# Moving preparations of the gated-linear-attention stage behind the norm's column sums in a two-layer trunk

## The chip, the cores and the metric

The kernel runs on one core of a Trainium2 chip. The metric is the device time of one execution in microseconds (us); lower is better. Engines are named as in the profile: PE is TensorE, PEld its weight load, DVE is VectorE, ACT is ScalarE, POOL is GpSimd, SP is SyncE, which issues nearly all DMAs (SPq is its queue).

## The reference

Two layers on a sequence of 1024 positions and a width of 1024, all float32. Layer 0 mixes tokens by forgetting attention, layer 1 by gated linear attention (GLA); each mixer is followed by a SwiGLU channel mixer (hidden width 2816). Every part has an RMS norm in front, modulated by a conditioning vector. The part that matters here is the seam between layer 0's channel mixer and layer 1's GLA:

```
x = x + g2 * swiglu(h, ffn_w_in[0], ffn_w_out[0])           # end of layer 0
h = modulate(rms_norm(x, norm1_g[1]), sh1, sc1)             # the norm in front of GLA
proj = h @ w_in
q, k, v, r, a_lr = split(proj, ...)                          # widths 512, 512, 1024, 1024, 16
log_alpha = log_sigmoid(a_lr @ w_a2 + b_a) / 16              # the low-rank gate
b = cumsum(log_alpha over a chunk of 64)
A = tril((q * exp(b)) @ (k * exp(-b)).T)                     # per chunk and head
o = A @ v + (q * exp(b)) @ state                             # and the recurrence of the state
o = rms_norm_per_head(o) * g_o * silu(r)
```

## The kernel before

The activations lie transposed: eight tiles of 128 features by 1024 positions, worked on in two halves of 512 positions. Every product of two float32 matrices is made of three matmuls (`mm3`, lines 241 to 243) on a high part (`hi`, a rounded copy that ScalarE casts) and a low part (`lo`, the rest, a subtraction on VectorE or GpSimd). So each weight that is loaded is also split: `load_w` (line 194) issues one DMA into a raw buffer, two casts on ScalarE (line 206) and four subtractions of a quarter each (line 209), of which the first `lo_p` (3 unless said otherwise) run on GpSimd and the rest on VectorE. `load_w16` (line 212) does the same for 16 columns, after a memset of its tile on GpSimd (line 217).

Weights are taken from one long list, `loads`. `feed.next()` (line 234) first starts loads until `depth` (here 3) are in hand and then gives the oldest. Raw buffers come from a ring of three, `wr`; split weights from a ring of eight slots, `ws`. A buffer is used again when its last reader is done.

The seam runs like this. `last_chunk` multiplies the last four hidden tiles (products named `f0e...`) in two halves; after each of eight features VectorE adds the product to x (line 1062), ScalarE squares it (line 577), and additions gather the squares (line 584). `rms_cols` then sums the columns on TensorE with one-column matmuls (`sp`, line 529, remembered in `sp_ins`), takes the root on GpSimd (line 533), and `rms_rows` spreads it over partitions (`rb`, line 541, remembered in `rb_ins`). `norm_half` makes h1 for that half: a product on VectorE (te, lines 554 and 559), casts on ScalarE (lines 555, 560, 561) and the low part, on VectorE for even features (line 556) and on GpSimd for odd ones (line 562). While the second half waits for its sums, GLA's value product of the first positions can already run on the first half of h1: `gv_body` (line 1599) makes one value tile of two blocks of 128 positions and splits it out of PSUM (tile `gvt`).

GLA's set-up stands between: memsets of a mask pair (`atz`), of the gate weight tile `w2t` and of the low-rank activation tile `aT`, the load and split of the low-rank weight `gla_w_a2` (raw tile `w2raw`), and the loads of the first value weights (`wv`), the low-rank input columns (`aw`, by `load_w16`), the first gate weight (dv 0 of head 0) and the first key weight. `a_body` and `gate_z` (lines 1588 and 1611) use them; `r_proj` makes the gate products `gr`, `head_front` the key and query products `gk` and `gqp`.

The program is traced in the order of the text. A planner then sets the order of instructions on each engine by simulating it: an instruction whose inputs and buffers are ready may go ahead of earlier ones that aren't, and where several are ready the one traced first goes. `with tc.issue_after(ins)` adds an edge that keeps those instructions of its block that run on the engine of `ins` behind `ins` in that engine's order. `sp_ins[-1]` and `rb_ins[-1]` are TensorE instructions.

In between, `ada1(t)` advances the modulation of the second layer (`ada_pair`, line 350) by a given amount: loads on SyncE (line 361), a product on ScalarE (lines 375 and 377) that is kept behind the ScalarE instruction traced `ADA_LAG` (6) before the last one, and an add on GpSimd (line 379). `gv_body` calls it once for each value tile.

Of the kernel before, what the change touches and what calls it, by code (L numbers as in the profile page):

```python
# [9 lines left out]
F32 = mybir.dt.float32  # L10
# [43 lines left out]
def trunk(ctx, tc, x, c, ada_w, ada_b, norm1_g, norm2_g, ffn_w_in, ffn_w_out,  # L54
          fox_w_in, fox_b_f, fox_w_out, gla_w_in, gla_w_a2, gla_b_a, gla_g_o,
          gla_w_out, final_g, out, dbg=None, stop=None):
    nc = tc.nc
# [9 lines left out]
    def ps_rings(*counts):  # L67
        r, i = [], 0
        for n in counts:
            r.append(Ring(psp, [f"b{j}" for j in range(i, i + n)]))  # L70
            i += n
        assert i <= 8
        return r
# [35 lines left out]
    def psl(t, n=1):  # L109
        return slice(t * P, (t + n) * P)  # L110

    def run(g):
        for _ in g:
            pass
# [4 lines left out]
    def weave(a, ta, b, tb, lags=None):  # L119


        ca = cb = 0.0
        a_on = b_on = True
        bb = nc.cur_bb.bb.instructions
        hist = {e: [] for e in lags or ()}
        while a_on or b_on:
            n = len(bb)
            if a_on and (not b_on or ca * tb <= cb * ta):
                r = next(a, None)
                a_on = r is not None  # L130
                ca += r or 0.0
                for e, h in hist.items():
                    new = [i for i in bb[n:] if i.engine == ENG[e]]
                    h.append(new[-1] if new else h[-1] if h else None)
            else:
                r = next(b, None)
                b_on = r is not None
                cb += r or 0.0
                for e, h in hist.items():
                    if len(h) > lags[e] and h[-1 - lags[e]] is not None:  # L140
                        for i in bb[n:]:
                            if i.engine == ENG[e]:
                                tc.add_manual_dep(i, h[-1 - lags[e]].name, mybir.DependencyInfo(
                                    mybir.DependencyClass.NoSync, mybir.DependencyReason.DATA), reason="order")
# [17 lines left out]
    def split(hi, lo, src):  # L162
        nc.scalar.copy(hi, src)  # L163
        nc.vector.tensor_sub(lo, src, hi.bitcast(F32))  # L164

    wr = Ring(big, names[0:3])
    ws = Ring(big, names[3:9])
# [58 lines left out]
    class Weights:  # L226
# [4 lines left out]
            self.got = deque()  # L231
            self.depth = 3

        def next(self):
            while self.loads and len(self.got) < self.depth:
                f, *a = self.loads.popleft()
                self.got.append(f(*a))
            return self.got.popleft()

    def mm3(ps, ah, al, bh, bl, start, stop):  # L240
# [11 lines left out]
    def proj_tok(ps, w2, hs, t):  # L252

        ts_ = psl(t)
        for k in range(8):
            w = w2[k // 4]
            mm3(ps, hs[k].hi[:, ts_], hs[k].lo[:, ts_], w.hi[:, k % 4, :], w.lo[:, k % 4, :], k == 0, k == 7)
            yield 0.33
# [145 lines left out]
    class Pace:  # L404
# [6 lines left out]
        def __call__(self, t):  # L411
            self.at += t
            while self.q and self.at >= 0:
                w = next(self.q[0], None)
                if w is None:
                    self.q.popleft()
                else:
                    self.at -= w
            if not self.q:
                self.at = 0.0  # L420
# [7 lines left out]
    def ada1_queue(js, acc, raws_):  # L428
        r = Cycle(raws_)
        for j in js:  # L430
# [6 lines left out]
                            fill=1e30, base=0, channel_multiplier=1)  # L437
# [5 lines left out]
                            fill=0.0, base=0, channel_multiplier=-1)  # L443
# [201 lines left out]
    def v_loads(wmat, lo):  # L645
        return [(load_w, wmat[psl(k0, 4), lo:lo + 256], f"wv{lo}_{k0}") for k0 in (0, 4)]
# [97 lines left out]
    def ffn_loads(l):  # L744

        blk = lambda gr, ab, *after: (op_block, l, gr, ab, *after)
        sums = lambda gr, *after: (op_sums, l, gr, *after)
        outs = lambda k0, kc, n: [(op_out, l, k0, kc, m0, i) for i in range(n) for m0 in range(0, D, 512 // kc)]
        g, u = GROUPS[:2]
        four = (A11, A21, A22, A12)  # L750
        r = [(op_first, l, g, A11, (g, four), (u, (A11, A12))), blk(g, A12), blk(g, A21), blk(g, A22, (u, (A21, A22)))]
        gs = GROUPS[1:] + OGROUPS
        for a, n in zip(gs, gs[1:] + [None]):
            first, then = ((n, four[:2]),), ((n, four[2:]),)
            if n is None:
                first = then = ()
            if a == u:
                r += [blk(a, A11), blk(a, A12, *first), blk(a, A21), blk(a, A22, *then)]
                continue
            r += [blk(a, A11), sums(a, *first)]  # L760
            if a[0] < 2:
                r += [blk(a, A11), (op_a12, l, a), blk(a, A21, *then), blk(a, A22), blk(a, A12)]
            else:
                r += [(op_s2, l, a), blk(a, A21, *then), blk(a, A12), blk(a, A22), blk(a, "s")]
        return r + outs(NFH - 4, 4, 2 + l)

    Wg = gla_w_in[0]
    loads = v_loads(W, 2 * D)
# [5 lines left out]
        loads += [a + (ws, 4) for a in fox]  # L774
    loads += out_loads(fox_w_out[0], 0, 4) + 2 * out_loads(fox_w_out[0], 4, 4)
    loads += ffn_loads(0)
    loads += v_loads(Wg, 1024) + [(load_w16, Wg[:, 3072:3088], "aw")]
    for h in range(4):
        if h:
            loads += v_loads(Wg, 1024 + h * 256)  # L780
# [5 lines left out]
    feed = Weights(loads)  # L786
# [774 lines left out]
    atz = Views(take(1), 2, [4, P], "atz")  # L1561
# [7 lines left out]
    nc.vector.memset(rm.rearrange("p (n c) -> p n c", c=P)[:, :, 0:1], 0.0)  # L1569
    og_d = tc.dram_tile([8, P, S], F32, name="og_d")  # L1570
    pj, atr, kvr, opr, trr = ps_rings(3, 1, 1, 2, 1)
    for v_ in atz.v:
        nc.gpsimd.memset(v_, 0.0)
    S_t = big.tile([P, 2, 2, 256], FR, tag=s_slot, name="S_t")
    on_t = big.tile([P, 2, 2, 256], F32, tag=on_slot, name="on_t")
    QS = 128 ** -0.5

    w2raw = wr([64, 512], F32, "w2raw")
    nc.sync.dma_start(w2raw[0:16, :], gla_w_a2[0])
    nc.sync.dma_start(w2raw[32:48, :], gla_w_a2[0])  # L1580
    w2t = big.tile([P, 2, 512], FR, tag=wslot, name="w2t")
    nc.vector.memset(w2t.bitcast(F32), 0.0)
    for r0 in (0, 32):
        split(w2t[r0:r0 + 16, 0, :], w2t[r0:r0 + 16, 1, :], w2raw[r0:r0 + 16, :])
    aT = big.tile([P, S], FR, tag=aslot, name="aT")
    nc.vector.memset(aT.bitcast(F32), 0.0)

    def a_body(aw, hf, bt):
        ps = pj([P, HALF], F32, f"aps{hf}")
# [9 lines left out]
    def gv_body(h, wv, tp):  # L1599
        ps = pj([P, 2, 256], F32, f"gv{h}{tp}")  # L1600
        for i in range(2):
            run(proj_tok(ps[:, i, :], wv, h1, 2 * tp + i))
        ada1(5.1)
        v = vr([P, 2, 2, 256], FR, f"gvt{h}{tp}")
        split(v[:, 0], v[:, 1], ps)
        return v
# [201 lines left out]
    def r_proj(h, gs, done):  # L1808
        wr_ = [None, None]
        for hf, dv in ((0, 0), (0, 1), (1, 0), (1, 1)) if h else ((0, 0), (1, 0), (0, 1), (1, 1)):  # L1810
# [6 lines left out]
            done.add((dv, hf))  # L1817
            yield 0.01

    wv = [feed.next(), feed.next()]  # L1820
    aw = feed.next()
    vt = [gv_body(0, wv, 0)]
    with tc.issue_after(sp_ins[-1]):
        vt.append(gv_body(0, wv, 1))
    with tc.issue_after(rb_ins[-1]):
        bt = gate_tiles(0)
# [123 lines left out]
```

## Time and profile before

| | |
|---|---|
| median of 3 runs | 2423.62 us (2423.13 to 2425.41) |
| profiled execution, its own time | 2419.46 us |
| span of the profiled execution | 2417.7 us |
| granted TensorE clock, mean | 0.995 |
| PE busy | 2369.4 us (98%) |
| DVE busy | 1680.8 us (70%) |
| ACT busy | 1194.4 us (49%) |
| POOL busy | 1181.0 us (49%) |

The times in a profile's rows count from the start of the span. A row of a timeline has the start, the duration, the engine, the line of the kernel, the operation, and output and inputs by the program's names; idle time in front of it and what ended it stand in brackets. A row of a table by stages has the stage, its length, the busy time of PE, PEld, DVE, ACT and POOL with their numbers of instructions, the granted TensorE clock, the share of the DMA engines and GB/s.

### The profile page before, as it was taken

The numbers are of one execution on the slowest core, as the hardware profiler recorded it, in microseconds if no ns is written. First come the engines' busy times: TensorE is split into PE (matmuls) and PEld (weight loads), VectorE is DVE, ScalarE is ACT, GpSimd is POOL, SyncE is SP. The second block draws the span as 40 slices with busy tenths as digits, with TensorE's granted clock in tenths as the row PEclk, the third lists the DMA queues.
The fourth block names the chain that finished last, engine by engine and source line by source line (L and its number), as shares of the span: only waits on it lengthen the run. The fifth ranks groups of instructions, "written<-read, shape, count | busy, mean of one in ns | idle before, by whom it ended". The sixth has DMA issues, their size and how long they took to land.

```text
span 2417.7 us, 36075 instructions
## 1 busy us (share of the span) xinstructions
PE 2369.4 (98%) x12338; PEld 2014.1 (83%) x12338; DVE 1680.8 (70%) x2819; ACT 1194.4 (49%) x2286; POOL 1181.0 (49%) x1041
## 2 busy tenths in 40 slices
PE   7999999999999999999999999999999999999998
PEld 6888888888888888888888788898888888888888
DVE  6577677676687777866797645546587767666787
ACT  4666565665454444445325856553343334345326
POOL 4344344433347878843263544552335656653362
PEclk9999999999999999999999999999999999999999
DMA  9233333123435555457655333444325444347664
GB/s 272 81 107 111 105 107 104 62 97 114 134 115 171 184 172 165 164 198 261 227 188 164 92 114 114 126 129 156 113 84 174 159 136 151 135 170 257 234 203 147
DMA packets 329504, 362.41 MB, mean 150 GB/s; under 512 B 24476, under 2 KB 252984, under 8 KB 329320
## 3 DMA queue, kind: packets, MB, share of 16 engines
q1 hardware_dynamic: 329128, 360.09, 45.6%
q8 instruction: 97, 1.59, 0.3%
q14 instruction: 87, 0.71, 0.1%
q10 hardware_dynamic: 192, 0.02, 0.0%
HBM read 269.78 MB, written 90.24 MB: 149 GB/s over the span
## 4 chain that ended last, share of the span: by engine, by line
PE 79%; DVE 6%; DMA 5%; ACT 3%; POOL 2%; issue 2%; SPq 2%; POOLq 0%; DVEq 0%; ACTq 0%
PE p_b L243 15%; PE p_b L242 15%; PE p_b L241 15%; PE o_b L969 2%; PE t_b L955 2%; PE qk_b L241 2%; PE qk_b L243 2%; PE qk_b L242 2%; DMA ad_s<-in_ada_w_dram 1%; PE s_b L924 1%; PE s_b L925 1%; SPq L361 1%; PE vps_b L242 1%; PE vps_b L241 1%; DVE o_s L164 1%
## 5 line engine op out<-in xcount | busy, mean ns | idle before, releaser
L164 DVE TENSOR_TENSOR o_s<-xv_s,o_s 128x512 fp32r<-128x512 f32 (+1 forms) x376 | 337.9, 902 | 82.0 <-ACT o_s L163 80.8
L163 ACT CAST o_s<-xv_s 128x512 fp32r<-128x512 f32 (+1 forms) x376 | 218.5, 588 | 317.6 <-PE p_b L243 247.7
L242 PE MATMUL p_b<-B,o_s 128*128 128x512 f32 x608 | 237.4, 390 | 0.0
L243 PE MATMUL p_b<-B,o_s 128*128 128x512 f32 x608 | 237.0, 390 | 0.0
L241 PE MATMUL p_b<-B,o_s 128*128 128x512 f32 x608 | 235.8, 390 | 0.0
L935 POOL TENSOR_SCALAR lp_s<-lp_s,st 128x128 f32<-128x128 f32 (+7 forms) x128 | 97.9, 769 | 267.5 <-DVE st L934 245.1
L702 POOL TENSOR_TENSOR ex_s<-xv_s,xv_s 128x512 f32<-128x512 f32 (+1 forms) x64 | 89.1, 1392 | 265.1 <-DMA xv_s<-in_ffn_w_in_dram 103.0
L241 PE MATMUL p_b<-T,o_s 128*128 128x512 f32 x480 | 186.7, 389 | 0.0
L242 PE MATMUL p_b<-T,o_s 128*128 128x512 f32 x480 | 186.7, 389 | 0.0
L243 PE MATMUL p_b<-T,o_s 128*128 128x512 f32 x480 | 180.7, 389 | 0.0
L243 PEld LDWEIGHTS p_b<-B,o_s 128*128 128x128 f32 x608 | 114.4, 188 | 23.7
L241 PEld LDWEIGHTS p_b<-B,o_s 128*128 128x128 f32 x608 | 114.4, 188 | 23.7
L242 PEld LDWEIGHTS p_b<-B,o_s 128*128 128x128 f32 x608 | 114.5, 188 | 23.6
L933 ACT ACTIVATE lp_s<-lp_s,st 128x128 f32<-128x128 f32 (+7 forms) x128 | 99.7, 779 | 63.8 <-DVE st L929 61.4
L163 ACT CAST pt_s<-t_b 128x512 fp32r<-128x512 f32 (+1 forms) x160 | 79.8, 549 | 72.9 <-PE t_b L955 72.3
L1307 DVE TENSOR_TENSOR ex_s<-ex_s,p_b 128x512 f32<-128x512 f32 x140 | 93.9, 681 | 27.6 <-PE p_b L243 27.5
L704 POOL TENSOR_TENSOR xv_s<-ex_s,xv_s 128x512 f32<-128x512 f32 (+1 forms) x64 | 84.8, 1325 | 55.2 <-DVE o_s L164 52.9
L164 DVE TENSOR_TENSOR pt_s<-t_b,pt_s 128x512 fp32r<-128x512 f32 (+1 forms) x160 | 96.7, 631 | 14.3 <-ACT pt_s L163 14.0
L242 PEld LDWEIGHTS p_b<-T,o_s 128*128 128x128 f32 x480 | 90.1, 188 | 18.7
L241 PEld LDWEIGHTS p_b<-T,o_s 128*128 128x128 f32 x480 | 90.1, 188 | 18.7
L243 PEld LDWEIGHTS p_b<-T,o_s 128*128 128x128 f32 x480 | 90.1, 188 | 18.7
L929 DVE CUSTOM_DVE_ANT_0 lp_s<-s_b,cum_s 128x512 f32<-128x512 f32 (+3 forms) x128 | 72.8, 571 | 40.8 <-PE t_b L955 19.7
(1950 smaller groups left out, 7510.2 us busy)
## 6 DMA issues: line engine op xcount, KB each, us to landing
xv_s<-in_ffn_w_in_dram SPq DMA_DIRECT2D x176, 256.0 KB, 3.1
hid_B<-x SPq DMA_DIRECT2D x70, 512.0 KB, 2.8
ad_s<-in_ada_w_dram SPq DMA_DIRECT2D x384, 64.0 KB, 2.0
hid_T<-x SPq DMA_DIRECT2D x36, 512.0 KB, 2.9
xv_s<-in_ffn_w_out_dram SPq DMA_DIRECT2D x96, 192.0 KB, 5.0
ada_s<-in_ada_w_dram SPq DMA_DIRECT2D x128, 128.0 KB, 2.7
xv_s<-in_ffn_w_out_dram SPq DMA_DIRECT2D x40, 256.0 KB, 2.7
T2o<-hid_T SPq DMA_DIRECT2D x18, 512.0 KB, 9.0
```

Of the source, the lines that this page charges most:

```text
L163: nc.scalar.copy(hi, src)
L164: nc.vector.tensor_sub(lo, src, hi.bitcast(F32))
L241: nc.tensor.matmul(ps, ah, bh, start=start, stop=False)
L242: nc.tensor.matmul(ps, ah, bl, start=False, stop=False)
L243: nc.tensor.matmul(ps, al, bh, start=False, stop=stop)
L702: nc.gpsimd.tensor_add(s1, a21, a22)
L704: nc.gpsimd.tensor_sub(a11, s1, a11)
L929: nc.vector.tensor_tensor_reduce(lp[:, k0:k1], ps, cm[:, k0:k1], 1.0, mcur, ALU.add, ALU.min, mnew)
L933: nc.scalar.activation(lp, lp, AF.Exp, bias=mcur, scale=-1.0, accum_out=st[:, qi, 2:3])
L935: nc.gpsimd.tensor_scalar(lp, lp, st[:, qi, 3:4], 1.0, op0=ALU.mult, op1=ALU.mult)
L955: nc.tensor.transpose(tp[:, i, :], lps[qi][:, psl(2 * b + jj)], ident)
L1307: nc.vector.tensor_add(d, d if src is None else dest(G, src), ps)
```

## The change

Five edits. The four low parts of each of head 0's two value weights are all made on GpSimd (`lo_p` 4). `feed.depth` is 1 while those weights are taken, so that `feed.next()` starts no further load there. The loads of `aw`, of the first gate weight and of the first key weight, and the set-up of the low-rank gate (now `a_prepare`), are traced after the first value tile instead of before it, inside the block that keeps the second value tile behind the column sums. The memset of `w2t` runs on GpSimd instead of VectorE. The memsets of `atz` and the load of `w2raw` move with the set-up, so the ring of raw buffers is taken in another order.

```diff
-        def next(self):
+        def fill(self):
             while self.loads and len(self.got) < self.depth:
                 f, *a = self.loads.popleft()
                 self.got.append(f(*a))
+
+        def next(self):
+            self.fill()
             return self.got.popleft()
...
-    loads += v_loads(Wg, 1024) + [(load_w16, Wg[:, 3072:3088], "aw")]
+    loads += [a + (ws, 4) for a in v_loads(Wg, 1024)] + [(load_w16, Wg[:, 3072:3088], "aw")]
...
-    for v_ in atz.v:
-        nc.gpsimd.memset(v_, 0.0)
     S_t = big.tile([P, 2, 2, 256], FR, tag=s_slot, name="S_t")
     on_t = big.tile([P, 2, 2, 256], F32, tag=on_slot, name="on_t")
     QS = 128 ** -0.5
 
-    w2raw = wr([64, 512], F32, "w2raw")
-    nc.sync.dma_start(w2raw[0:16, :], gla_w_a2[0])
-    nc.sync.dma_start(w2raw[32:48, :], gla_w_a2[0])
     w2t = big.tile([P, 2, 512], FR, tag=wslot, name="w2t")
-    nc.vector.memset(w2t.bitcast(F32), 0.0)
-    for r0 in (0, 32):
-        split(w2t[r0:r0 + 16, 0, :], w2t[r0:r0 + 16, 1, :], w2raw[r0:r0 + 16, :])
     aT = big.tile([P, S], FR, tag=aslot, name="aT")
-    nc.vector.memset(aT.bitcast(F32), 0.0)
+
+    def a_prepare():
+        w2raw = wr([64, 512], F32, "w2raw")
+        nc.sync.dma_start(w2raw[0:16, :], gla_w_a2[0])
+        nc.sync.dma_start(w2raw[32:48, :], gla_w_a2[0])
+        nc.gpsimd.memset(w2t.bitcast(F32), 0.0)
+        for r0 in (0, 32):
+            split(w2t[r0:r0 + 16, 0, :], w2t[r0:r0 + 16, 1, :], w2raw[r0:r0 + 16, :])
+        nc.vector.memset(aT.bitcast(F32), 0.0)
+        for v_ in atz.v:
+            nc.gpsimd.memset(v_, 0.0)
...
+    feed.depth = 1
     wv = [feed.next(), feed.next()]
-    aw = feed.next()
     vt = [gv_body(0, wv, 0)]
     with tc.issue_after(sp_ins[-1]):
+        feed.depth = 3
+        feed.fill()
+        aw = feed.next()
+        a_prepare()
         vt.append(gv_body(0, wv, 1))
     with tc.issue_after(rb_ins[-1]):
         bt = gate_tiles(0)
```

## The prediction

> **What bounds the kernel now.** I read the page first, then the busy time of the stage that the diff touches, then what TensorE waited for there, then that stretch engine by engine.
>
> ```profile
> span 2417.7 us, 36075 instructions
> PE 2369.4 (98%) x12338; PEld 2014.1 (83%) x12338; DVE 1680.8 (70%) x2819; ACT 1194.4 (49%) x2286; POOL 1181.0 (49%) x1041
> ```
>
> ```profile
> 1308.40:1334.40 26.00, 22.01 (x154) 20.41 (x152) 18.29 (x27) 13.48 (x23) 9.82 (x10) 0.93 0.56 170
> ```
>
> ```profile
> PE gr_b L241 <- DVE gvt_s L164: 1.7, 1, 1.7
> PE gv_b L243 <- DVE h1l L556: 1.2, 1, 1.2
> PE sp_b L529 <- DVE se_s L584: 0.7, 1, 0.7
> PE gv_b L243 <- POOL h1l L562: 0.4, 1, 0.4
> ```
>
> TensorE is busy for 98% of the span, so time can only come from its few gaps, and the touched stretch (1308.40 to 1334.40 us, from the last product of the first channel mixer to the first gate product) holds 26.00 - 22.01 = 3.99 us of them. The four waits of the second view are all of it: 0.4 and 1.2 us inside the first value tile, 0.7 us ahead of the second half's column sums, 1.7 us ahead of the gate product. What VectorE (DVE) did before those sums:
>
> ```profile
> 1297.40 0.99 DVE L209 TENSOR_TENSOR wv_0l_s<-wv_s,wv_0h_s 128x256 fp32r<-128x256 f32 x1
> ...
> 1299.20 0.73 DVE L554 SCALAR_TENSOR_TENSOR te_s<-x,amul,rb_b 128x512 f32<-128x512 f32 x1
> ...
> 1309.94 1.36 DVE L164 TENSOR_TENSOR aw_s<-aw_s,aw_s 128x128 fp32r<-128x128 f32 x1
> 1313.57 0.41 DVE L209 TENSOR_TENSOR w_l_s<-w__s,w_h_s 128x256 fp32r<-128x256 f32 x1
> 1314.14 0.91 DVE L1582 MEMSET w2t<- 128x1024 f32 x1 [0.17 <-issue]
> 1315.21 0.91 DVE L1586 MEMSET aT<- 128x1024 f32 x1 [0.16 <-issue]
> 1316.05 0.62 DVE L1062 SCALAR_TENSOR_TENSOR x<-f0e11871p_b,modc,x 128x512 f32<-128x512 f32 x1
> 1316.59 0.67 DVE L584 TENSOR_TENSOR se_s<-se_s 128x512 f32<-128x512 f32 x1
> 1317.19 1.38 DVE L164 TENSOR_TENSOR w2t<-w2raw_s,w2t 16x512 fp32r<-16x512 f32 x2
> 1327.18 0.75 DVE L554 SCALAR_TENSOR_TENSOR te_s<-x,amul,rb_b 128x512 f32<-128x512 f32 x1 [6.00 <-PE rb_b L541]
> ```
>
> ```profile
> 1317.32 3.51 PE L529 MATMUL sp_b<-ones,se_s 128*128 128x1 f32 x30 [0.67 <-DVE se_s L584]
> ...
> 1341.86 0.40 PE L1618 MATMUL z_b<-aT,w2t 128*128 128x512 f32 x1
> ...
> 1356.87 0.39 PE L243 MATMUL gk_b<-h1h,w_l_s 128*128 128x512 f32 x1
> ```
>
> The first columns are start and duration; what ended an idle time stands in brackets. The reader is to see that five preparations (value-weight pieces, aw, w_l, two memsets) stand ahead of the last residual update (1316.05) and the last addition of squares (1316.59), for which the column sums wait, and that VectorE then idles 6.00 us until 1327.18, when it could have done them.
>
> **The change, part by part.** *Value weights.* All eight low pieces go to GpSimd. VectorE gets to its first normalising product at 1297.40 instead of 1299.20: 1.80 us. GpSimd's bill:
>
> ```profile
> 1299.84 1.44 POOL L209 TENSOR_TENSOR wv_4l_s<-wv_s,wv_4h_s 128x256 fp32r<-128x256 f32 x2
> 1302.49 0.94 POOL L217 MEMSET aw_s<- 128x1024 f32 x1
> ...
> 1306.51 2.96 POOL L209 TENSOR_TENSOR w_l_s<-w__s,w_h_s 128x256 fp32r<-128x256 f32 x3
> 1309.43 3.00 POOL L562 TENSOR_TENSOR h1l<-te_s,h1h 128x512 fp32r<-128x512 f32 x2
> 1327.48 1.30 POOL L379 TENSOR_TENSOR ad_s<-ad_s,ad_s 128x512 f32<-128x512 f32 x1 [5.32 <-ACT ad_s L377]
> ...
> 1340.22 1.30 POOL L562 TENSOR_TENSOR h1l<-te_s,h1h 128x512 fp32r<-128x512 f32 x1 [0.70 <-ACT h1h L561]
> 1355.26 8.68 POOL L209 TENSOR_TENSOR w_l_s<-w__s,w_h_s 128x256 fp32r<-128x256 f32 x9
> ```
>
> ```profile
> 1301.31 0.38 SPq L198 DMA_DIRECT2D w__s<-in_gla_w_in_dram  x1
> ```
>
> ```profile
> 1325.35 0.72 ACT L375 ACTIVATE ad_s<-ad_s,cblk 128x512 f32<-128x512 f32 x1 [1.71 <-DMA ad_s<-in_ada_w_dram]
> ...
> 1335.40 0.62 ACT L561 CAST h1h<-te_s 128x512 fp32r<-128x512 f32 x1
> ```
>
> Two pieces more at 1.44 / 2 = 0.72 us are 1.44 us on a queue whose low parts of h1 (1309.43) TensorE already waits for. If the three w_l pieces (2.96 us) leave the place ahead of them, GpSimd is ahead by 1.52 us; if not, behind by 1.44.
>
> *The w2t memset* goes from VectorE to GpSimd: 1315.21 - 1314.14 = 1.07 us off VectorE, about the 0.94 us of the aw memset (same shape) onto GpSimd, where it lies free unless it stands in front of the last low part.
>
> *The rest of a_prepare, the aw and w_l loads* are only traced later, behind the first value tile. The `issue_after` block ties TensorE instructions alone (the column sums are TensorE's), and none of these is one. Program order by itself holds little back: the aT memset ran at 1315.21 although the second half's products, traced before it, ran at 1327.18. So their effect lies between nothing and 1.36 + 0.41 + 0.84 (aT, 1315.21 to 1316.05) = 2.61 us more off VectorE; I count nothing, and the w_l pieces on GpSimd as moved, since they are ready last. If they do go behind, the 6.00 us of idle VectorE hide 1.36 + 0.41 + 0.91 + 1.38 = 4.06 us; the first reader of w2t and aT is at 1341.86.
>
> *Raw buffers.* The three rotate one place: aw takes the one that w2raw had and can load earlier, the first gate weight takes the first value weight's (free within GpSimd's pieces, about as at 1301.31), w2raw follows aw. On SyncE's queue the two small w2raw loads stand later, nothing that TensorE needs before 1341.86 behind them. Between -0.5 and +0.5 us; I take zero.
>
> *The modulation's first product* (1325.35) is tied behind the seventh-last ScalarE instruction traced so far; that was a w2t cast and becomes an h1 cast of the second half (as at 1335.40). Its adds (1.30 us each) move into GpSimd's second run of h1 low parts. Free if they come after 1340.22, up to 2.3 us if not; I take zero.
>
> *Sum.* The last addition of squares ends 1.80 + 1.07 = 2.87 us earlier: the sums could start at 1317.32 - 2.87 = 1314.45. TensorE ends the first value tile at 1317.32 - 0.67 = 1316.65, and without the waits of 1.2 and 0.4 us at 1315.05, so it, not VectorE, is late next. Gain: 1317.32 - 1315.05 = 2.27 us, say 2.3. From there broadcast, products and value tile follow at the same distances, with the 1.7 us wait kept. On the profiled execution: 2417.7 - 2.3 = 2415.4 us of span, 2419.46 - 2.3 = 2417.16 us of time. That execution is 4.16 us below the median of the runs, 2423.62, so the forecast in medians is **2421.3**.
>
> Contention is weighed against that. The value piece at 1297.40 took 0.99 us with GpSimd at work beside it, the same shape at 1313.57 took 0.41. The Trainium skill, GPSIMD Engine Reference, Key points, has GpSimd share its SBUF interfaces with VectorE, in contention with instructions of two SBUF inputs: it speaks against moving pieces there, and the trace agrees (0.99 against 0.41). By that rule 1.44 + 0.94 us more of GpSimd would stretch VectorE's low parts by up to 59% of that, an estimated 1.4 us, and the sum would be 1.5 instead of 2.3 us.
>
> The clock is the other open size:
>
> ```profile
> 1320.80:1326.20 5.40, 5.40 (x35) 5.40 (x35) 0.32 (x3) 1.86 (x3) 1.02 (x1) 0.68 0.54 157
> 1764.00:1770.00 6.00, 6.00 (x25) 4.93 (x24) 0.85 (x2) 0.06 (x1) 1.02 (x1) 0.72 0.00 0
> 668.00:676.00 8.00, 8.00 (x55) 7.30 (x55) 1.18 (x3) 0.91 (x3) 2.33 (x3) 1.00 0.12 47
> ```
>
> After the burst of one-column sums the granted clock was 0.68 here and 0.72 in the second channel mixer, but 1.00 in the first: between 0 and 5.40 x 0.32 = 1.7 us, by chance of where the burst falls. I keep it as it is and put 1.7 us into the range. The Trainium skill, TensorE: Matmul & The Clock Gate, section on the HAM clock gate, says that the gate looks at a free-running window of about 3.4 us; by that rule a shift of 2.3 us may as well remove the slow stretch, for an estimated 1.7 us more.
>
> **The rivals.**
> *All of it moves behind.* Then VectorE is 2.87 + 2.61 = 5.48 us ahead, the value tile is evacuated in time, and the 1.7 us wait goes too, and with luck most of the slow clock: 2.3 + 1.7 + 1.4 = 5.4 us, **2418.2**. For: 6.00 us idle wait for that work. Against: nothing but position in the trace moves it.
> *It doesn't do what it says.* The planner puts everything where it was ready before; GpSimd has 1.44 us more ahead of both low parts, TensorE's waits there become 0.4 + 1.44 = 1.84 us and, at the last low part, about 0.4 us (this one ends 1.44 us later, but TensorE also comes to it later), as much as the 2.3 us that go; with the memset before the last low part 0.9 us more. **2423.9**. For: the aT memset at 1315.21.
> *Slower: GpSimd's queue becomes the bound.* To that 0.9 us come three adds of 1.30 us in front of the low part at 1340.22, which then ends at 1345.4 where the value tile reads it at about 1343.1 (2.3 us), and two more ahead of the key weights at 1355.26, whose first piece (0.96 us) is read at 1356.87: 1355.26 + 0.96 + 2.60 = 1358.82, 1.95 us late. Together 5.2 us: **2428.8**. It decides once the adds run later than the cast at 1335.40. For: the tie above. Against: GpSimd idled 5.32 us before 1327.48, so there is room.
>
> **How the numbers follow.** Forecast 0.32 (of it 0.08 below 2418.8, with clock or last wait gone as well), all behind 0.24 (0.02 of it not below), no effect 0.16, GpSimd bound 0.28 (0.03 of it under 2428.5). A change of 0.2%, 4.85 us, is about what a measurement of this kernel can tell from none. Faster: 0.08 + 0.22 = 0.30; slower: 0.25; within: 0.45. The forecast's own range is 2419.6 (1.7 us of clock) to 2423.6; with the others, 2417.2 to 2429.0.
>
> **What would show it.** Right: the first normalising product at the broadcast's end, no wait of the column sums on L584, their burst at about 1315, no w_l piece between GpSimd's low parts. Wrong: TensorE waiting for POOL h1l by more than 0.4 us; GpSimd adds between the low parts of the second half; gk waiting for w_l. If the sums start 2 us earlier and the time is the same, a wait later in head 0 took it.

## The result, and the profile after

The changed kernel took 2437.13 us (median of 7 runs, 2429.84 to 2439.25) against 2425.41 us of the kernel before (7 runs): a ratio of 1.0039, 95% interval 1.0028 to 1.0050. The ratio is estimated from all runs and lies near that of their means; the two medians alone would give 1.0048. On other runs later (after_2) it was 1.0042, 1.0027 to 1.0056. It is slower, by some 10 us. The forecast was 2421.3, with 2417.2 to 2429.0 around it and a chance of 0.25 for slower.

The profiled execution has a span of 2437.3 us, 19.6 more than before's. From the page of after:

```profile
span 2437.3 us, 36077 instructions
PE 2380.5 (98%) x12338; PEld 2024.3 (83%) x12338; DVE 1678.5 (69%) x2816; ACT 1191.3 (49%) x2286; POOL 1179.3 (48%) x1044
```

Not all of the 19.6 us comes from the change. The last product of the first channel mixer, `f0e11871p`, starts at 1308.12 us before and at 1314.67 after: 6.55 us that are lost before the moved steps run, at a lower clock (0.990 against 0.995 over the execution). It is the profile of before that is early there: those of all other runs have that product at 1310.4 to 1316.0. So I measure one stretch, called the stage below: from the start of that last product to the first key product (`gk`). The table by stages has one row for it in each profile, before first, after second:

```profile
1308.10:1355.90 47.80, 43.69 (x292) 39.98 (x291) 28.82 (x42) 30.42 (x53) 19.71 (x17) 0.96 0.33 103
```

```profile
1314.70:1373.50 58.80, 50.34 (x294) 46.55 (x293) 28.24 (x40) 29.91 (x51) 22.61 (x20) 0.83 0.27 82
```

The stage is 11.0 us longer, close to what the medians show (11.7). TensorE does the same matmuls in both, but for two gate products (`z`, some 0.46 us by their starts) that stand ahead of the first key product in after alone. Yet it is busy 6.65 us more (50.34 - 43.69), at a granted clock of 0.83 in place of 0.96, and idle 4.35 us more (8.46 against 4.11). The idle time is these waits (waits of TensorE, after; us in total, times, longest):

```profile
PE gv_b L244 <- DVE gvt_s L164: 3.9, 1, 3.9
PE sp_b L532 <- DVE se_s L587: 2.1, 1, 2.1
PE gv_b L246 <- POOL h1l L565: 1.8, 1, 1.8
PE gr_b L244 <- DVE gvt_s L164: 0.6, 1, 0.6
```

The wait ahead of the column sums did not go; it grew from 0.7 to 2.1 us. What VectorE and GpSimd did before it (timeline of after):

```profile
1304.19 0.75 DVE L557 SCALAR_TENSOR_TENSOR te_s<-x,amul,rb_b 128x512 f32<-128x512 f32 x1
...
1309.22 1.61 DVE L559 SCALAR_TENSOR_TENSOR h1l<-te_s,modc,h1h 128x512 fp32r<-128x512 f32 x1
...
1311.41 3.28 DVE L559 SCALAR_TENSOR_TENSOR h1l<-te_s,modc,h1h 128x512 fp32r<-128x512 f32 x2
...
1316.46 1.22 DVE L559 SCALAR_TENSOR_TENSOR h1l<-te_s,modc,h1h 128x512 fp32r<-128x512 f32 x1
...
1318.26 1.26 DVE L209 TENSOR_TENSOR w_l_s<-w__s,w_h_s 128x256 fp32r<-128x256 f32 x1
1319.44 1.36 DVE L164 TENSOR_TENSOR aw_s<-aw_s,aw_s 128x128 fp32r<-128x128 f32 x1
1320.97 0.91 DVE L1589 MEMSET aT<- 128x1024 f32 x1 [0.16 <-issue]
1321.81 0.62 DVE L1065 SCALAR_TENSOR_TENSOR x<-f0e11871p_b,modc,x 128x512 f32<-128x512 f32 x1
1322.35 0.67 DVE L587 TENSOR_TENSOR se_s<-se_s 128x512 f32<-128x512 f32 x1
```

```profile
1311.13 3.01 POOL L565 TENSOR_TENSOR h1l<-te_s,h1h 128x512 fp32r<-128x512 f32 x2
1314.10 3.02 POOL L209 TENSOR_TENSOR w_l_s<-w__s,w_h_s 128x256 fp32r<-128x256 f32 x3
1317.07 0.95 POOL L1586 MEMSET w2t<- 128x1024 f32 x1
1317.98 2.68 POOL L565 TENSOR_TENSOR h1l<-te_s,h1h 128x512 fp32r<-128x512 f32 x2
```

The reader is to see that w_l, aw and the aT memset still stand ahead of the last residual update (1321.81) and the last addition (1322.35), as before, and the w_l pieces and now the memset on GpSimd ahead of the low parts of h1 (1317.98). Only the split of w2t stands behind, where it stood before too (1317.19). That the low parts come later shows as 1.8 us of wait in place of 0.4.

The rest comes from an order that no line of the diff states. Matmuls on TensorE in the stage, in the order of the two traces (the first value tile has 48; the 16 sums are the 32 one-column matmuls of the profile):

```
before: gv 10, first sum 1, gv 38, sums 15, gv 32, rb, gv 16, aps, gr 24, gv 16, z 2, gv 32, aps, gv 48, gk ...
after:  gv 14, first sum 1, gv  9, sums 15, gv 26, rb, gv 47, aps, gr 24, gv 12, z 2, gv 36, aps, gv 36, z 2, gv 12, gk ...
```

All sums but the first stand behind 48 products of the first value tile before and behind 23 after, so TensorE comes to them earlier and waits, with work in hand that stands behind them. Then (timeline and table by stages of after):

```profile
1323.08 6.56 PE L532 MATMUL sp_b<-ones,se_s 128*128 128x1 f32 x30 [2.14 <-DVE se_s L587]
```

```profile
1323.00:1329.70 6.70, 6.62 (x31) 6.62 (x32) 1.89 (x5) 1.33 (x3) 0.00 (x0) 0.50 0.21 82
1360.00:1373.50 13.50, 9.60 (x54) 9.05 (x53) 2.39 (x4) 6.84 (x17) 4.14 (x4) 0.75 0.15 39
```

The burst of sums ran at half clock throughout, 6.56 us for what took 3.51. And 40 us later a wait stands that before has none of: TensorE needs the PSUM tile of the third value tile back (3.9 us), and its evacuation begins with a cast on ScalarE that stands behind the exponentials and two products of the modulation:

```profile
1361.82 0.39 ACT L1674 ACTIVATE t_s<-b_s,dec 128x128 f32<-128x128 f32 x1
1362.11 1.32 ACT L380 ACTIVATE ad_s<-ad_s,cblk 128x512 f32<-128x512 f32 x2
1363.33 0.56 ACT L163 CAST gvt_s<-gv_b 128x512 fp32r<-128x512 f32 x1
```

In the kernel before the same cast comes ahead of the exponentials (timeline of before):

```profile
1347.01 0.57 ACT L163 CAST gvt_s<-gv_b 128x512 fp32r<-128x512 f32 x1
1347.60 1.28 ACT L1668 ACT_TABLE_LOAD   x1
```

### The profile page after: what moved, and what is told of

Same layout as the page of the kernel before. It is cut to its first block, busy times and chain, and to the rows that moved or that the text cites. A ratio compares the mean times of both kernels' runs of the same rounds, so it can differ in the third digit from the quotient of the medians.

```text
span 2437.3 us, 36077 instructions
## 1 busy us (share of the span) xinstructions
PE 2380.5 (98%) x12338; PEld 2024.3 (83%) x12338; DVE 1678.5 (69%) x2816; ACT 1191.3 (49%) x2286; POOL 1179.3 (48%) x1044
## 4 chain that ended last, share of the span: by engine, by line
PE 84%; DVE 4%; DMA 3%; ACT 3%; POOL 2%; issue 2%; SPq 1%; ACTq 0%; DVEq 0%; POOLq 0%
PE p_b L246 16%; PE p_b L245 16%; PE p_b L244 16%; PE o_b L972 2%; PE t_b L958 2%; PE qk_b L244 2%; PE qk_b L246 2%; PE qk_b L245 2%; PE s_b L927 1%; PE s_b L928 1%; DMA ad_s<-in_ada_w_dram 1%; PE vps_b L245 1%; PE vps_b L244 1%; SPq L364 1%; PE vps_b L246 1%
```

## The experiments

The theory to be tested: the place of the column sums in TensorE's order is the cause, and the waits, the clock and the late evacuation follow from it. The rivals: GpSimd's and VectorE's new work is the cause by itself; the late tracing is; the clock was only unlucky. The column "sums behind" leaves out the first sum, which stands behind 10 or 14 products. All figures of the stage are from one profiled execution each; times are medians, ratios go against runs of the kernel before beside them on the same chip, whose medians lay between 2425.41 and 2427.74 us.

| kernel | sums behind | stage us | PE busy | PE idle | clock | time us (runs) | ratio, 95% interval |
|---|---|---|---|---|---|---|---|
| before | 48 | 47.80 | 43.69 | 4.11 | 0.96 | 2425.41 (7) | 1 |
| after | 23 | 58.80 | 50.34 | 8.46 | 0.83 | 2437.13 (7) | 1.0039, 1.0028 to 1.0050 |
| after_2 | 23 | 58.40 | 49.49 | 8.91 | 0.85 | 2437.09 (5) | 1.0042, 1.0027 to 1.0056 |
| values | 48 | 50.30 | 44.92 | 5.38 | 0.93 | 2425.75 (12) | 0.9991, 0.9981 to 1.0001 |
| late | 48 | 49.50 | 46.75 | 2.75 | 0.90 | 2424.95 (11) | 0.9994, 0.9985 to 1.0003 |
| values_memset | 23 | 57.90 | 49.56 | 8.34 | 0.85 | 2433.72 (11) | 1.0028, 1.0019 to 1.0037 |
| no_memset | 48 | 46.40 | 43.51 | 2.89 | 0.96 | 2421.78 (8) | 0.9977, 0.9967 to 0.9987 |
| no_memset_2 | 48 | 47.80 | 45.18 | 2.62 | 0.93 | 2426.74 (11) | 1.0003, 0.9994 to 1.0013 |
| burst_held | 48, the second 23 | 51.80 | 46.24 | 5.56 | 0.90 | 2427.78 (11) | 1.0004, 0.9995 to 1.0013 |
| burst_held2 | 48 | 50.00 | 46.77 | 3.23 | 0.90 | 2428.77 (11) | 1.0002, 0.9991 to 1.0012 |
| evac_first | 23 | 53.30 | 47.99 | 5.31 | 0.87 | 2429.49 (11) | 1.0011, 1.0002 to 1.0020 |
| early | 23 | 60.10 | 49.54 | 10.56 | 0.86 | 2439.06 (6) | 1.0050, 1.0035 to 1.0064 |
| clock_kept | 23 | 64.60 | 53.18 | 11.42 | 0.87 | 2441.10 (5) | 1.0060, 1.0048 to 1.0073 |
| clock_filled | 23 | 56.90 | 49.38 | 7.52 | 0.94 | 2435.88 (5) | 1.0034, 1.0021 to 1.0047 |
| behind | 31 to 35 | 45.70 | 44.88 | 0.82 | 0.93 | 2422.96 (10) | 0.9982, 0.9972 to 0.9991 |
| behind_2 | 31 to 35 | 44.20 | 43.27 | 0.93 | 0.96 | 2422.93 (12) | 0.9983, 0.9973 to 0.9992 |
| behind_held | 48 | 45.50 | 43.23 | 2.27 | 0.96 | 2424.46 (11) | 0.9990, 0.9981 to 0.9999 |

**One part at a time.** `values` is the kernel before with the value pieces on GpSimd alone:

```diff
-    loads += v_loads(Wg, 1024) + [(load_w16, Wg[:, 3072:3088], "aw")]
+    loads += [a + (ws, 4) for a in v_loads(Wg, 1024)] + [(load_w16, Wg[:, 3072:3088], "aw")]
```

> The kernel before, with one edit: all eight low parts of head 0's value weights on GpSimd. Measured by the stage from the end of the first channel mixer's last product to the first key product: 47.4 us before, 58.5 us after. Theory A (the column sums' burst is planned ahead of the first value tile's second half, which takes two edits together; TensorE then idles and its clock halves): the burst stays behind the whole tile, stage 46 to 49 us, time within 2.5 us of before. Theory B (the late tracing, its ring of raw buffers and the modulation's tie cost the time): stage 47 us, as before. Theory C (GpSimd's extra pieces alone cost it, by the wait for its h1 low parts): wait for GpSimd about 1.8 us, stage 52 us or more.

`late` is the changed kernel with the value pieces and the w2t memset back where they were, so that only the later tracing is left:

```diff
-    loads += [a + (ws, 4) for a in v_loads(Wg, 1024)] + [(load_w16, Wg[:, 3072:3088], "aw")]
+    loads += v_loads(Wg, 1024) + [(load_w16, Wg[:, 3072:3088], "aw")]
...
-        nc.gpsimd.memset(w2t.bitcast(F32), 0.0)
+        nc.vector.memset(w2t.bitcast(F32), 0.0)
```

> The changed kernel without the moves to GpSimd: value weights' last pieces and the w2t memset on VectorE, only the late tracing is left. Theory A (the order of the burst, set off by values and memset together): the burst stays behind the whole first value tile, stage from the first mixer's last product to the first key product 47 to 49 us (47.8 before, 58.9 after), time within 3 us of before; with the values' pieces (no_memset) it was 46.4 us. Theory B (late tracing costs): stage 52 us or more.

Neither alone moves the time by 0.1%, and in neither do the sums from the second on change their place, though the stages, 50.3 and 49.5 us, came out above the forecasts' 49. The value pieces alone are worth nothing. In the profile of `values` nothing waits any more ahead of the burst of sums (only the first sum, earlier in the tile, waits 0.5 us), but the wait for VectorE's low part inside the value tile grows from 1.2 to 2.7 us. One low part took 7.35 us there, and the same instruction 0.74 us later on, when GpSimd was idle (timeline of `values`):

```profile
1309.33 7.35 DVE L556 SCALAR_TENSOR_TENSOR h1l<-te_s,modc,h1h 128x512 fp32r<-128x512 f32 x1
...
1318.53 0.74 DVE L556 SCALAR_TENSOR_TENSOR h1l<-te_s,modc,h1h 128x512 fp32r<-128x512 f32 x1
```

```profile
1309.01 3.84 POOL L562 TENSOR_TENSOR h1l<-te_s,h1h 128x512 fp32r<-128x512 f32 x3
1312.77 2.14 POOL L209 TENSOR_TENSOR w_l_s<-w__s,w_h_s 128x256 fp32r<-128x256 f32 x3
1314.84 1.30 POOL L562 TENSOR_TENSOR h1l<-te_s,h1h 128x512 fp32r<-128x512 f32 x1
```

The long one ended at 1316.68, half a microsecond behind the last of this unbroken run of GpSimd's. It put the last addition 10.45 us behind the last mixer product, against 8.47 in the kernel before, and took away what the moved pieces had gained. After_2 has such a part of 4.91 us, after has none: the stretch differs between executions of one kernel.

`values_memset` is the kernel before with the value pieces and the memset on GpSimd, and nothing traced later:

```diff
-    nc.vector.memset(w2t.bitcast(F32), 0.0)
+    nc.gpsimd.memset(w2t.bitcast(F32), 0.0)
```

> The kernel before, with two edits: the value weights' low parts on GpSimd and the w2t memset on GpSimd; nothing is traced later, the raw buffers rotate as before. Theory A: the burst is planned ahead of the second half of the first value tile, TensorE idles about 4 us ahead of it, the granted clock drops to about 0.5 in the burst, stage 56 to 60 us, time 8 to 13 us above before. Theory B: stage 47 to 49 us, time as before. Theory C: as with the values alone, 1 us more.

It has the changed kernel's early place of the sums and nearly its loss, 1.0028. Its waits (waits of TensorE):

```profile
PE gv_b L241 <- DVE gvt_s L164: 3.8, 1, 3.8
PE sp_b L529 <- DVE se_s L584: 3.5, 1, 3.5
PE gr_b L241 <- DVE gvt_s L164: 1.1, 1, 1.1
```

So the two moves onto GpSimd turn the order together; the later tracing is not needed for it. Why the planner turns it just then is not shown: the ready times that it reckoned with are not on record. `no_memset`, the changed kernel with this one line on VectorE again, has the sums in their old place:

```diff
-        nc.gpsimd.memset(w2t.bitcast(F32), 0.0)
+        nc.vector.memset(w2t.bitcast(F32), 0.0)
```

> The changed kernel, with the w2t memset back on VectorE; late tracing and the value weights' pieces stay as changed. Theory A: the burst is back behind the whole first value tile, stage 46 to 49 us, time within 3 us of before. Theory B: stage 55 us or more, time 8 us or more above before, since all that is traced late still is. Theory C: stage 52 us or more.

It gave 0.9977, faster than the kernel before. On another chip it gave 1.0003:

> The changed kernel with the w2t memset back on VectorE, a second time on other runs. Theory (the order of the kernel before is restored, VectorE has the value pieces less): 2420.5 to 2423.5 us, ratio to the kernel before 0.997 to 0.999. Rival (the first measurement was a lucky spread of the clock): 2424 to 2426.5 us, ratio 0.999 to 1.000.

The two intervals don't overlap: the interval of one set of runs does not hold what differs between sets. The profiled spans are 5.8 us apart (2420.8 and 2426.6), of which the stage has 1.4; 1.7 lie ahead of it and 2.1 up to the next channel mixer's sums, at the mean granted clocks of 0.9943 and 0.9925 over all runs. That this kernel beats the one before is left open; that it has none of the changed kernel's 0.4% is shown twice.

**The order taken back.** `burst_held` and `burst_held2` are the changed kernel with edges that keep the sums from the third, or from the second on, behind the whole first value tile (`sp_all` holds the sums' matmuls):

```diff
+    tile0 = last_of("P")
+    for i in sp_all[2:]:        # burst_held2: sp_all[1:]
+        tc.add_manual_dep(i, tile0.name, mybir.DependencyInfo(
+            mybir.DependencyClass.NoSync, mybir.DependencyReason.DATA), reason="order")
```

> The changed kernel, with the column sums (from the third on) kept behind the last matmul of the first value tile in TensorE's order by order edges; nothing else differs. Theory A: the 2.1 us wait ahead of the burst goes, the clock in the burst is 1.0, stage 48 to 51 us, time 6 to 10 us below the changed kernel. Theory B and C: the stage stays at 55 us or more, for the late tracing and GpSimd's pieces are still there.

> As burst_held, but from the second column sum on: in burst_held the second sum still stood inside the tile's first half and TensorE waited 2.8 us at it. Theory A: no wait ahead of the burst of more than 0.5 us, stage 46 to 49 us, time as with no_memset (0.2% below before), since then all that is left of the change is what was meant. Rival: GpSimd's memset and pieces cost on their own: the wait for its h1 low parts (1.8 us) stays and the stage is 50 us or more.

Both are level with the kernel before (1.0004, 1.0002), with every moved step left in. The 3.9 us wait is gone in both without an edge on it. In `burst_held` the second sum still waits 2.8 us inside the tile; in `burst_held2` nothing waits ahead of the sums, and the 1.8 us for GpSimd's low part are left. Its expectation, a stage of 46 to 49 us and 0.2% below before, missed; as its rival had it, that wait stays, and the stage is 50.0 us.

`evac_first` leaves the sums early and only has the cast of the third value tile ahead of the exponentials:

```diff
-    gate_exps(0, bt, (0,), to0)
     vt.append(gv_body(0, wv, 2))
+    with tc.issue_after(last_of("A")):
+        gate_exps(0, bt, (0,), to0)
```

> The changed kernel, with the first half's gate exponentials traced after the third value tile and kept behind that tile's cast in ScalarE's order. Theory A takes the 3.9 us wait for that cast, and the halved clock after it, for a consequence of the early burst that comes on top: the wait goes, the stage is 52 to 54 us instead of 58.9, the 2.1 us wait and the slow burst stay. Rival: the cast is not what the fourth value tile waits for last, another release comes as late (the low part on VectorE, or the low-rank product's bank), and the stage stays above 57 us.

The 3.9 us wait falls to 0.6, the stage from 58.8 to 53.3 us and the ratio to 1.0011; what is left over before's 47.8 is the wait ahead of the sums (2.8 us), that for GpSimd's low part (1.8 us) and the clock (0.87). So most of the loss runs over the late cast, and the early sums with their own waits leave about 0.1%.

**The order alone.** `early` is the kernel before with the first value tile's products from the 24th on tied behind the sums, and every preparation left on its engine:

```diff
+    n0 = len(nc.cur_bb.bb.instructions)
     vt = [gv_body(0, wv, 0)]
+    mm0 = [i for i in nc.cur_bb.bb.instructions[n0:] if i.engine == ENG["P"]]
+    for i in mm0[23:]:
+        tc.add_manual_dep(i, sp_ins[-1].name, mybir.DependencyInfo(
+            mybir.DependencyClass.NoSync, mybir.DependencyReason.DATA), reason="order")
```

> The kernel before with one thing changed: the first value tile's products from the 24th on are tied behind the column sums, so that TensorE's order is that of the changed kernel (sums behind 23 products); all preparations stay where they were, on their engines. Theory (that order is the cause): waits ahead of the sums of 2 to 4 us and one of 3 to 4 us for the third value tile's evacuation, a granted clock of 0.8 to 0.88 over the stage, stage 56 to 60 us against 47.8, time 2432 to 2437 us, ratio 1.002 to 1.004. Rival (GpSimd's and VectorE's new work is the cause, and the order only goes along): stage 48 to 51 us, time 2425 to 2428 us, ratio within 0.1% of 1.

1.0050: as large a loss as the changed kernel's, within the intervals, without any of the diff; the time, 2439.06 us, is above the 2432 to 2437 that the theory said. The stage, its first slow part, and the waits (table by stages, then waits of TensorE):

```profile
1315.40:1375.50 60.10, 49.54 (x294) 45.57 (x293) 29.46 (x42) 31.11 (x53) 20.75 (x18) 0.86 0.31 90
```

```profile
1323.10:1336.70 13.60, 11.78 (x55) 11.78 (x56) 3.75 (x8) 4.03 (x7) 1.02 (x1) 0.50 0.57 167
```

```profile
PE sp_b L529 <- DVE se_s L584: 3.7, 1, 3.7
PE gv_b L241 <- DVE gvt_s L164: 3.4, 1, 3.4
PE gr_b L241 <- DVE gvt_s L164: 1.7, 1, 1.7
PE gv_b L243 <- DVE h1l L556: 1.2, 1, 1.2
PE gv_b L243 <- POOL h1l L562: 0.5, 1, 0.5
```

The wait ahead of the sums, 13.6 us at half clock that begin inside it, and the wait for the third value tile's evacuation all come with the one edge. The rival, that the new work on GpSimd is the cause by itself, wanted 2425 to 2428 us and falls.

**The clock.** Is the half clock a matter of TensorE's idle time? `clock_kept` puts 17 products that nothing reads in the place of the two waits around the sums. It missed its purpose: their PSUM tile came from a ring whose bank still held the last mixer product, so that they waited 3.60 us for the last residual update and made a new wait.

```diff
+    def idle_work(n, behind, ahead, nm):
+        ps = opr([P, HALF], F32, f"idle{nm}")
+        n1 = len(nc.cur_bb.bb.instructions)
+        with tc.issue_after(behind):
+            for k in range(n):
+                nc.tensor.matmul(ps, h1[0].hi[:, 0:P], h1[0].hi[:, 0:HALF], start=k == 0, stop=k == n - 1)
...
+    idle_work(8, mm0[16], mm0[17:18], "a")
+    idle_work(9, mm0[22], sp_all[1:], "b")
```

> The changed kernel with 17 extra 512-column matmuls whose result nobody reads, 8 ahead of the matmul that waits for GpSimd in the first value tile and 9 ahead of the burst (17 x 0.227 = 3.9 us, as long as the two waits); order and everything else as changed. If the halved clock is caused by TensorE's idling there: the waits are filled, the burst lasts 3.5 us instead of 6.6, the granted clock in it is 1.0, the stage falls by 3 to 5 us although TensorE does more. Rival, the clock halves from the one-column matmuls of the burst themselves, as it did in the kernel before without such a wait: the burst or the matmuls behind it stay slow and the stage is unchanged or longer.

`clock_filled` is the same in banks that are free then:

```diff
-        ps = opr([P, HALF], F32, f"idle{nm}")
+        ps = psp.tile([P, HALF], F32, tag=bank, name=f"idle{nm}")
...
-    idle_work(8, mm0[16], mm0[17:18], "a")
-    idle_work(9, mm0[22], sp_all[1:], "b")
+    idle_work(8, mm0[16], mm0[17:18], "a", "b7")
+    idle_work(9, mm0[22], sp_all[1:], "b", "b6")
```

> The changed kernel with 8 and 9 products of 128x512 that nothing reads, put on TensorE in place of the wait inside the first value tile (1.8 us) and of the wait ahead of the sums (2.1 us), into PSUM banks b7 and b6, which nothing else uses then. They cost about 17 x 0.23 = 3.9 us if they hide no wait, nothing if the waits hide them. Theory (idle TensorE ahead of the one-column sums halves the clock): granted clock 0.9 or more in the burst, which lasts 3.4 to 4.5 us in place of 6.6, stage 53 to 56 us with the 3.9 us wait for the third value tile still there, time 2431 to 2434 us. Rival (the burst itself, or the execution as a whole, halves the clock): burst above 5.5 us again, stage 58 us or more, time 2437 us or more.

Timeline and waits of TensorE in `clock_filled`:

```profile
1316.56 2.00 PE L1838 MATMUL idlea<-h1h 128*128 128x512 f32 x8
...
1319.38 2.23 PE L1838 MATMUL idleb<-h1h 128*128 128x512 f32 x9
1322.37 3.63 PE L533 MATMUL sp_b<-ones,se_s 128*128 128x1 f32 x30 [0.76 <-DVE se_s L589]
```

```profile
PE gv_b L244 <- DVE gvt_s L164: 3.9, 1, 3.9
PE gr_b L244 <- DVE gvt_s L164: 2.9, 1, 2.9
PE sp_b L533 <- DVE se_s L589: 0.8, 1, 0.8
```

The burst took 3.63 us, not 6.56, and TensorE's own work in the stage 49.38 - 2.00 - 2.23 = 45.15 us, 5.2 less than after's. So the idle time of the two waits makes most of the clock loss in the profile. In the time it can't be told: the intervals of `clock_filled` (1.0021 to 1.0047) and of the changed kernel overlap. For the stage is only 1.9 us shorter: 4.23 us are the fill, and the wait for the first value tile's evacuation grew from 0.6 to 2.9 us, since TensorE came there sooner and VectorE did not. The forecast of this run, 53 to 56 us and 2431 to 2434, missed that.

**What the change set out to do, with edges.** `behind` is the changed kernel with the memset on VectorE and the later steps really tied, on their engines, behind the last addition (`marks["add"]`), the last residual update and the first half's last low part on GpSimd:

```diff
-        nc.gpsimd.memset(w2t.bitcast(F32), 0.0)
+        nc.vector.memset(w2t.bitcast(F32), 0.0)
...
-        feed.depth = 3
-        feed.fill()
-        aw = feed.next()
-        a_prepare()
+        with tc.issue_after(marks["add"]), tc.issue_after(marks["x"]), tc.issue_after(marks[("low", 0)]):
+            feed.depth = 3
+            feed.fill()
+            aw = feed.next()
+            a_prepare()
```

> The changed kernel with the w2t memset on VectorE, and with the aw cast, the first gate weight, w2raw and both clears really tied (order edges on every engine) behind the last addition of squares, the last residual update and the first half's last low part on GpSimd, as the text of the change says they stand. Theory (TensorE's order and its clock decide, and VectorE's cover is worth little once the preparations fit): no wait for GpSimd's low parts ahead of the sums, but the sums are planned in part at 31 to 35 products of the first value tile, so a wait of about 1 us inside them stays; stage from the last mixer product to the first key product 46 to 49 us, time 2421 to 2425 us, not below the kernel without the memset (2421.8). Rival of the prediction (all of it moves behind): the wait ahead of the sums and that for the value tile's evacuation both go, stage 43 to 44 us, time about 2418 us.

`behind_held` has the edges of `burst_held2` as well:

> The same with the column sums from the second one on held behind the whole first value tile. Theory: no wait in front of the sums, the burst stands behind 48 products as in the kernel before, stage 45 to 48 us with 1.5 to 4 us of clock loss, time 2420 to 2424 us. Rival (all of it behind is worth its full 5.4 us): 2418 us. If holding costs what it saves: equal to the kernel just before, within 1 us.

> The variant with the preparations tied behind the last addition, the last update and the low part, on other runs. Theory (3.3 us of waits less than the kernel before, the clock as it falls): 2421 to 2425 us, ratio 0.997 to 0.9995. Rival (a lucky spread of the clock, as with the kernel without the memset): 2425 to 2427 us, ratio 0.9995 to 1.0005.

`behind` is faster than both kernels, by the same in two sets of runs, both on one chip: 0.9982 and 0.9983. Its stage, its slow part and all of its waits:

```profile
1312.20:1357.90 45.70, 44.88 (x293) 41.62 (x292) 26.00 (x41) 29.36 (x51) 21.39 (x19) 0.93 0.33 98
```

```profile
1318.00:1322.00 4.00, 4.00 (x27) 4.00 (x25) 2.24 (x4) 0.00 (x0) 0.00 (x0) 0.65 0.84 259
1322.00:1328.00 6.00, 6.00 (x37) 6.00 (x37) 2.62 (x6) 1.82 (x3) 1.51 (x1) 0.66 0.43 102
```

```profile
PE sp_b L533 <- DVE se_s L589: 0.7, 1, 0.7
```

Idle time falls from 4.11 to 0.82 us; the clock still drops in the burst of sums, with next to no wait ahead of it. Here the sums may stand behind 31 to 35 products, for what they wait for is early enough. With the sums held (`behind_held`) TensorE waits 2.1 us for the value tile's evacuation, and the median is 1.5 us higher (2424.46 against 2422.96), but the intervals overlap: that holding costs time here is not shown.

**The size.** After_2 asked whether the changed kernel's loss was an unlucky clock:

> The changed kernel itself, on other runs. Theory (waits and order are planned, so the loss repeats; only its clock part varies): 2431 to 2439 us, ratio 1.002 to 1.005, 3.9 us wait for the third value tile's evacuation again. Rival (the first measurement was a bad spread of the clock): 2425 to 2429 us, ratio below 1.001.

It repeats: 1.0042, the 3.9 us wait too.

## Why the prediction was wrong

- **The step that failed** is in the sum: "From there broadcast, products and value tile follow at the same distances". It took TensorE's order as given. With both moves onto GpSimd the planner put the sums 25 products earlier, presumably because it took their inputs to be ready earlier, and everything behind them fell into another order, down to a cast on ScalarE 40 us later. `early` shows this order alone to cost 1.0050, `burst_held2` its removal to leave 1.0002; without the late cast it is 1.0011 (`evac_first`). No rival of the prediction had it; its slower rival put the price on GpSimd's adds and the key weights, and no product waits for key weights in the trace of after.
- **VectorE's relief** was put at 2.87 us, 1.80 for the value pieces and 1.07 for the memset. Measured from the start of the last mixer product, the first normalising product came 10.48 us ahead of it in place of 8.92 (1.56 us gained), but the last addition only 0.79 us sooner (7.68 us behind it, against 8.47; in after_2's profile, with its low part of 4.91 us, 8.32). Between them VectorE took 18.16 us against 17.39, though the memset was gone: the four low parts took 6.11 us against 5.24 (1.02, 1.19, 1.27 and 1.76), the w_l piece 1.26 against 0.41. So the relief was mis-sized by 2.1 us, and about 1.7 of that is stretch beside GpSimd's work. The Trainium skill, GPSIMD Engine Reference, Key points, says that GpSimd shares its SBUF interfaces with VectorE, in contention with instructions of two SBUF inputs; these rows agree, and the estimate of 1.4 us made by it should have gone into the sum.
- **The place of w_l on GpSimd.** I counted the three pieces as moved, "since they are ready last". They stood ahead of the low parts (1314.10), and the memset with them (1317.07). The rival in which the change doesn't do what it says priced TensorE's wait for that at 1.84 us; it was 1.79. So of the two waits inside the tile that the sum let go, 0.4 and 1.2 us, the first grew. The rival's total, 2423.9, missed, for the same reason as the forecast's.
- **The clock** was allowed 1.7 us for chance, one stretch of 3.4 us at half clock. TensorE's busy time in the stage grew by 6.65 us (5.80 in the profile of after_2), some 0.46 of it for the two gate products. Chance alone does not explain that: `clock_filled` brings back 5.2 by filling two waits, and two profiles of one kernel differ by 0.8 to 1.7 us. But before's 43.69 us lies at the good end of the kernels with the sums behind 48 products (43.2 to 46.8), so a part of the 6.65 us may be luck of that profile.
- **Right:** that the later tracing by itself holds little back (`late`, 0.9994), that the two small loads and the raw buffers cost nothing that can be seen, and that VectorE's idle time behind the sums would hide all of it if it did go there. The rival "all of it moves behind" said 5.4 us for that; tied with edges, with the memset on VectorE, it is 3.8 and 4.8 us (2426.79 - 2422.96, 2427.74 - 2422.93). The wait for the evacuation went as it said, most of the slow clock did not.

## What to carry to other kernels

Where a planner sets the order, moving work off the engine that feeds an instruction can move that instruction, and with it the order of everything behind it: compare the two programs' orders on the engine that bounds the kernel before adding up durations. An early place for an instruction is only good if its inputs really come by then; where they don't, hold it with an edge, or bring the inputs forward with edges (both were level or faster here). Work moved to GpSimd should be priced with the stretch that it puts on VectorE beside it, which can be far more than a share (7.35 us for an instruction of 0.74), and a ratio of a few tenths of a per cent should be repeated on other runs and another chip before it is believed.

## What the runs showed of the hardware

In short stretches the granted clock was 1.00 or 0.50; the values between them in the tables are means over both (table by stages of before, then of after):

```profile
1320.90:1321.10 0.20, 0.20 (x3) 0.20 (x3) 0.16 (x2) 0.00 (x0) 0.00 (x0) 1.00 1.15 348
1321.15:1324.50 3.35, 3.35 (x18) 3.35 (x17) 0.03 (x1) 1.14 (x2) 1.01 (x1) 0.50 0.55 153
```

```profile
1314.70:1319.30 4.60, 2.81 (x22) 2.44 (x20) 4.60 (x5) 2.29 (x4) 4.60 (x6) 1.00 0.31 126
1319.35:1332.95 13.60, 11.46 (x52) 11.16 (x53) 5.53 (x10) 1.86 (x3) 2.33 (x2) 0.50 0.45 144
1363.75:1370.50 6.75, 5.83 (x27) 5.83 (x28) 1.96 (x3) 1.34 (x3) 1.73 (x2) 0.50 0.30 78
```

In after the clock fell at about 1319.3, behind the wait of 1.79 us for GpSimd's low part and ahead of the wait of 2.14 us, and it stayed low through that wait, the burst of one-column sums (6.56 us) and some products of the value tile. In `early` it fell 1.8 us into the wait of 3.7 us. In before it fell at about 1321.1, though TensorE had not waited since 1317.32; what it ran there was the burst. The Trainium skill, TensorE: Matmul & The Clock Gate, section on the HAM clock gate, has the clock halved after at least one idle window of about 3.4 us; the trace has shorter waits and still the half clock, so here one-column matmuls and waits between matmuls seem to count as idle together. That reading is argued from the windows, not shown by a run of its own.
